# FFN2's gate and up of a hybrid decoder layer, with seven block products for eight

## The chip, the core and the metric

The kernel runs on one core of one Trainium2 chip. The metric is the device time of one execution in microseconds (us). The engines are TensorE (PE; its weight loads are listed as PEld), VectorE (DVE), ScalarE (ACT), GpSimd (POOL) and SyncE (SP), which issues the DMAs. Matmuls accumulate in PSUM; all else lies in SBUF.

## The reference

One decoder layer over 1024 tokens (and 16 meta tokens) of width 1024. The change touches the last sub-layer alone:

```python
def rms_norm(x, g):
    y = xf * lax.rsqrt(jnp.mean(xf * xf, axis=-1, keepdims=True) + EPS)
    return (y * g.astype(jnp.float32)).astype(x.dtype)
def swiglu(x, w_gate, w_up, w_down):
    return (jax.nn.silu(x @ w_gate) * (x @ w_up)) @ w_down
...
h = h + 0.5 * swiglu(rms_norm(h, g_ffn2[l]), w2_gate[l], w2_up[l], w2_down[l])
```

Gate and up are products of 1024 features, 1024 tokens and 2816 columns each; down goes back from 2816 to 1024. All is float32.

## The kernel before, in words

Features or columns lie on the 128 partitions and tokens along the free dimension, so `h` is eight tiles of 128 x 1024. Every float32 operand x of a matmul is split into a rounded part `hi` (ACT copies it to fp32r) and a rest `lo` (x - hi, a subtraction on POOL, on DVE where named), and each product is three passes (`PASS`): hi hi, hi lo, lo hi.

The layer runs FFN1, the mixer's projections, attention (in an order written out by a table of due times), the output projection (16 products `out_proj`, eight feature tiles by two token halves) and FFN2. Outside attention the framework's scheduler sets the order on each engine; the engines then run their queues strictly in that order.

FFN2 has 22 column blocks of 128 for gate and up. `FFN.gu` makes one block for one half of the tokens (chunk c, 512 tokens) with 24 matmuls of 512 columns: three passes over eight feature tiles (line 289). Its input u is h times the gain g, split in `scaled_u` (line 207 on ACT, 208 on DVE). The norm's factor 1/rms of each token comes later: `gate` multiplies the PSUM result by it (line 301), takes silu (302) and multiplies by the factor again for up (303, POOL); `up` multiplies up's result with that (317) and splits the product (318, 319). Since the factor comes late, the first blocks need only h. `rstd_cols` and `rstd_rows` make it: small matmuls with ones (line 218), a chain of tiny DVE operations (225, 135 to 142), a copy (236), four transposes on PE (240) and a copy (241).

`down` (line 327) takes two blocks at a time: for each of eight output tiles and two halves, six matmuls, then one DVE operation that adds half of it to h (line 333). Weights come as whole blocks of 512 KB (line 174, SP's queue) and are split whole, 128 x 1024 (182 on ACT, 183 on POOL; the same lines split the output projection's weights).

Three other lines are named in the rows: 198 sums the squares of h on POOL, 1218 adds an `out_proj` result in PSUM to h on DVE, and 1113 makes a `lo` part in attention on DVE from two SBUF tensors.

Of the kernel before, what the change touches and what calls it, by code (L numbers as in the profile page):

```python
# [1405 lines left out]


# [75 lines left out]
```

## Time and profile before

| | us |
|---|---|
| three runs | 2260.83, 2263.03, 2263.74 |
| median of the runs | 2263.03 |
| profiled execution, its own time | 2260.83 |
| profiled execution, span from first to last instruction | 2259.1 |

The profiled execution is the fastest of the three runs; 1.73 us of its time lie outside the span. The page gives PE 97% of the span, DVE 41%, ACT 30% and POOL 36%. In the stretches FFN1 fills the time to about 780 us, the projections to about 1060, attention to about 1430, the output projection to about 1520, and FFN2 the rest. Times in the rows are us from the span's start; PEclk is the clock that TensorE was granted, 1.00 being full speed.

### The profile page before, as it was taken

To read this page: it belongs to the slowest core of one execution; us is meant where nothing else is said; L and a number is where in the kernel's file an instruction comes from. 1 tells how busy PE (TensorE), PEld (TensorE's weight loads), DVE (VectorE), ACT (ScalarE), POOL (GpSimd) and SP (SyncE) were. 2 spreads that over 40 slices of the span, in tenths; PEclk is the share of its full clock that TensorE was granted. 3 is DMA by queue.
4 is the path that set the end of the run, shared out by engine and by line. 5 is a ranking of instruction groups with operands and counts; after the bars stand their busy time and mean duration, and the time that the engine had idled before them with its cause. 6 is when DMAs were issued, how large, how long until landed. Compare 5 with 4: busy or idle time off the path is not lost.

```text
span 2259.1 us, 29231 instructions
## 1 busy us (share of the span) xinstructions
PE 2181.1 (97%) x11667; PEld 1881.2 (83%) x11667; DVE 926.1 (41%) x1933; ACT 676.4 (30%) x1181; POOL 817.1 (36%) x609
## 2 busy tenths in 40 slices
PE   7999999999999979988988999999999999999999
PEld 7999999999999967856666777778888888888887
DVE  8332222232223776654666776273222222222222
ACT  5211211111211443332665777342111111111110
POOL 4433433333433621421332223374433333433331
PEclk9999999999999999998998999999999999999999
DMA  4111111111110114354332212231111111111101
GB/s 161 57 53 41 57 38 56 38 38 57 57 38 30 40 38 116 111 193 149 115 107 64 58 49 89 65 103 47 55 39 56 37 38 56 56 47 47 47 19 75
DMA packets 96095, 149.10 MB, mean 66 GB/s; under 512 B 25512, under 2 KB 66056, under 8 KB 95960
## 3 DMA queue, kind: packets, MB, share of 16 engines
q1 hardware_dynamic: 95672, 147.12, 19.9%
q8 instruction: 91, 1.49, 0.3%
q14 instruction: 44, 0.36, 0.0%
q10 hardware_dynamic: 288, 0.13, 0.0%
HBM read 119.32 MB, written 27.77 MB: 65 GB/s over the span
## 4 chain that ended last, share of the span: by engine, by line
PE 87%; DVE 5%; DMA 5%; ACT 2%; issue 1%; SPq 0%; POOL 0%; DVEq 0%; ACTq 0%; POOLq 0%
PE t L289 11%; PE s L289 11%; PE m L289 11%; PE o L289 10%; PE m L327 5%; PE t L327 5%; PE o L327 5%; PE s L327 5%; PE s L549 5%; PE o L1134 4%; PE s L1086 3%; DMA b<-q_f 2%; PE m L1009 2%; PE t L549 1%; DVE b L208 1%
## 5 line engine op out<-in xcount | busy, mean ns | idle before, releaser
L183 POOL TENSOR_TENSOR b<-b,b 128x1024 fp32r<-128x1024 f32 (+2 forms) x161 | 387.1, 2412 | 705.7 <-ACT b L182 698.2
L182 ACT ACTIVATE b<-b 128x1024 fp32r<-128x1024 f32 (+2 forms) x166 | 172.3, 1051 | 626.1 <-PE t L327 210.3
L289 PE MATMUL s<-b,b 128*128 128x512 f32 (+3 forms) x1368 | 267.0, 351 | 9.8 <-DVE b L205 9.8
L289 PE MATMUL t<-b,b 128*128 128x512 f32 (+3 forms) x1368 | 268.1, 351 | 0.2
L289 PEld LDWEIGHTS s<-b,b 128*128 128x128 f32 x1368 | 234.1, 190 | 33.4 <-ACT b L182 8.2
L289 PEld LDWEIGHTS t<-b,b 128*128 128x128 f32 x1368 | 234.0, 188 | 25.1 <-DVE b L208 0.7
L289 PE MATMUL m<-b,b 128*128 128x512 f32 (+3 forms) x1272 | 251.1, 353 | 0.0
L289 PE MATMUL o<-b,b 128*128 128x512 f32 (+3 forms) x1272 | 247.8, 350 | 0.0
L289 PEld LDWEIGHTS m<-b,b 128*128 128x128 f32 x1272 | 220.7, 189 | 23.0
L289 PEld LDWEIGHTS o<-b,b 128*128 128x128 f32 x1272 | 218.0, 189 | 21.9
L319 POOL TENSOR_TENSOR b<-a,b 128x512 fp32r<-128x512 f32 (+3 forms) x110 | 119.1, 1083 | 173.5 <-ACT b L318 173.5
L303 POOL TENSOR_TENSOR s<-s,b 128x512 f32<-128x512 f32 (+3 forms) x110 | 118.5, 1079 | 136.9 <-ACT s L302 136.9
L318 ACT ACTIVATE b<-a 128x512 fp32r<-128x512 f32 (+3 forms) x110 | 60.2, 548 | 304.6 <-DVE a L317 304.5
L1016 DVE TENSOR_REDUCE b<-m 128x1 f32<-128x144 f32 (+7 forms) x224 | 111.9, 507 | 92.6 <-PE m L1012 64.3
L327 PE MATMUL m<-b,b 128*128 128x512 f32 (+3 forms) x666 | 146.2, 350 | 0.0
L327 PE MATMUL t<-b,b 128*128 128x512 f32 (+3 forms) x660 | 143.7, 350 | 0.0
L327 PE MATMUL o<-b,b 128*128 128x512 f32 (+3 forms) x654 | 142.3, 350 | 1.3 <-DVE rv L225 1.3
L327 PE MATMUL s<-b,b 128*128 128x512 f32 (+3 forms) x660 | 142.1, 350 | 0.0
L302 ACT ACTIVATE s<-s 128x512 f32<-128x512 f32 (+3 forms) x110 | 60.2, 549 | 266.7 <-DVE s L301 266.6
L1086 PE MATMUL s<-b,b 70*128 70x512 f32 (+4 forms) x480 | 129.5, 377 | 6.1 <-ACT b L1101 3.8
L549 PE MATMUL s<-b,b 128*128 128x512 f32 (+3 forms) x504 | 124.4, 399 | 7.1 <-DVE t L615 3.6
L1111 POOL TENSOR_TENSOR s<-b,b 128x512 fp32r<-128x512 f32 (+2 forms) x48 | 59.2, 1233 | 180.2 <-ACT b L1105 115.4
(323 smaller groups left out, 3104.2 us busy)
## 6 DMA issues: line engine op xcount, KB each, us to landing
b<-in_w1g_dram SPq DMA_DIRECT2D x22, 512.0 KB
b<-in_w1u_dram SPq DMA_DIRECT2D x22, 512.0 KB
b<-in_w1d_dram SPq DMA_DIRECT2D x22, 512.0 KB
b<-in_w2g_dram SPq DMA_DIRECT2D x22, 512.0 KB
b<-in_w2u_dram SPq DMA_DIRECT2D x22, 512.0 KB
b<-in_w2d_dram SPq DMA_DIRECT2D x22, 512.0 KB
b<-in_wout_dram SPq DMA_DIRECT2D x16, 512.0 KB
b<-in_winf_dram SPq DMA_DIRECT2D x12, 512.0 KB
```

The source lines that it names most:

```text
L182: nc.scalar.activation(out=hi[:, :n], in_=raw[:, :n], func=ACTF.Copy)
L183: (eng or nc.gpsimd).tensor_tensor(out=lo[:, :n], in0=raw[:, :n], in1=hi_of(hi[:, :n]), op=ALU.subtract)
L289: nc.tensor.matmul(p[:, :w], lhsT=wt[a][:, kd, :], rhs=self.u[b][kd][:, c0:c0 + w], start=(n == 0), stop=(n == 23))
L302: nc.scalar.activation(out=s[:, :w], in_=s[:, :w], func=ACTF.Silu)
L303: nc.gpsimd.tensor_tensor(out=s[:, :w], in0=s[:, :w], in1=r, op=ALU.mult)
L318: nc.scalar.activation(out=ah, in_=a[:, :w], func=ACTF.Copy)
L319: nc.gpsimd.tensor_tensor(out=al, in0=a[:, :w], in1=hi_of(ah), op=ALU.subtract)
L327: nc.tensor.matmul(p[:, :w], lhsT=self.tiles["d", f][a][:, dc * 128:(dc + 1) * 128], rhs=self.act[f][b][:, c0:c0 + w], start=(n == 0), sto ...
L549: nc.tensor.matmul(p[:rows, :n], lhsT=u[b][2 * j + k][:, c0:c0 + rows], rhs=wt[g, j][a][:, k, :n], start=(i == 0), stop=(i == 23))
L1016: nc.vector.tensor_reduce(smax[n % 2][:, i, z:z + 1], s[:, :w], axis=AX.X, op=ALU.max)
L1086: nc.tensor.matmul(s[:, o:o + w], lhsT=kb[:kk, kc:kc + 128], rhs=qa[:kk, q0:q0 + w], start=(z == 0), stop=end and not mw)
L1134: nc.tensor.matmul(O[:rows, c], lhsT=v, rhs=hl[p][:r, o:o + w], start=(k == 0 and z == 0), stop=(end and z == 2))
```

## The change

FFN2 no longer uses `FFN`. Its input is normalised first: `unorm` multiplies h, gain and factor (two SBUF tensors on DVE), and the result is split like any operand. The token halves are U11 and U12 for the first four feature tiles, U21 and U22 for the last four.

Column blocks 0 and 1 are made as before, 24 matmuls each for a half (`plain`). From block 2 on `chain` takes two blocks f, f+1 at a time as a 2 x 2 problem: two column blocks, two halves of the features, two halves of the tokens. Seven products of 12 matmuls (three passes over four feature tiles) take the place of eight, in the Winograd form of Strassen's scheme: the weight sums are S1 = W21 + W22, S2 = S1 - W11, S3 = W11 - W21, S4 = W12 - S2; the input sums are T1 = U12 - U11, T2 = U22 - T1, T3 = U22 - U12, T4 = U21 - T2, each split into hi and lo. The input sums are made once; the weight sums for each pair of blocks. The seven results are put together by seven additions on DVE for each of gate and up (one of them begins as a copy on ACT).

Weights come as quarters of 128 x 512 (256 KB) into four raw buffers; a quarter is loaded when the one four before it has been used up. An operand of a product is split (128 x 512) into one of four slots when the product four before it is done. The down weights share both.

```diff
-    CH2 = [(0, 512), (512, 512)]
-    uu = ([oh[k] for k in range(KD)], [ol[k] for k in range(KD)])
-    rbc2 = blk(37)
-    ffn2 = FFN(h, uu, CH2, oring, (w2g, w2u, w2d), [(28, 29), (38, 39), (43, 44)],
-               rbc2, ps)
...
+    REG, RAWB, ACTB = [28, 29, 38, 39], [43, 44], [40, 41, 42, 45]
+    TB = ([24, 25, 26, 27], [30, 31, 32, 33], [34, 35, 36, 37])
...
+    def split2(hi, lo, src, eng=None):
+        nc.scalar.activation(out=hi, in_=src, func=ACTF.Copy)
+        (eng or nc.gpsimd).tensor_tensor(out=lo, in0=src, in1=hi_of(hi), op=ALU.subtract)
+    def dsub(out, a, b):
+        nc.vector.tensor_tensor(out=out, in0=a, in1=b, op=ALU.subtract)
...
+    def unorm(out, k, c):
+        nc.vector.scalar_tensor_tensor(out=out, in0=h[k][:, 512 * c:512 * c + 512],
+                                       scalar=gc[:, G_FFN2 + k:G_FFN2 + k + 1], in1=rbc[c],
+                                       op0=ALU.mult, op1=ALU.mult)
+    def half0(k):
+        t = ht("t", bufs=3)
+        unorm(t, k, 0)
+        split2(*u_half(k, 0), t)
...
+        def plan(self, items):
+            for key, slot in items:
+                k, f, z = key
+                if slot is None:
+                    slot = REG[self.turn % 4]
+                    self.at[key] = self.turn
+                    self.turn += 1
+                self.items.append((key, slot))
+                if k == "d" or f < 2:
+                    self.loads.append(key)
+                    self.uses[key] = 1
...
+        def load_ahead(self):
+            while self.nl < len(self.loads):
+                n = self.nl
+                if n > 3 and self.uses[self.loads[n - 4]]:
+                    return
...
+        def source(self, key):
+            k, f, z = key
+            q = lambda n: self.use(k, f, n)
+            if z == "S1":
+                t = self.sums[k, f, z] = ht("acc")
+                nc.vector.tensor_tensor(out=t, in0=q(21), in1=q(22), op=ALU.add)
+            elif z == "S2":
+                t = self.sums[k, f, z] = ht("acc")
+                dsub(t, self.sums[k, f, "S1"], q(11))
+                w = self.sums[k, f, "S3"] = q(11)
+                dsub(w, w, q(21))
+            elif z == "S3":
+                q(11)
+            elif z == "S4":
+                w = self.sums[key] = q(12)
+                dsub(w, w, self.sums[k, f, "S2"])
+            else:
+                return q(z)
+            return self.sums[key]
...
+        def done(self, key):
+            t = self.at[key] + 4
+            for i, (k, _) in enumerate(self.items):
+                if self.at.get(k) == t:
+                    self.split_to(i + 1)
...
     for k in range(len(EC["OP"]), 16):
         o_split(k + 3)
         o_load(k + 5)
-        if k > 13:
-            ffn2.split_to(k - 13)
         out_proj(k, ps)
-        if k >= 8:
-            scaled_u(h, k - 8, 0, 512, G_FFN2, *uu)
+        if k == 8:
+            y0 = rstd_cols(ps, 512, accs[0])
         if k == 9:
-            rstd_rows(ps, 0, 512, rstd_cols(ps, 512, accs[0]), rbc2)
-    for kd in range(KD):
-        scaled_u(h, kd, 512, 512, G_FFN2, *uu)
-    ffn2.split_to(4)
...
-    ffn2.run(first2, last2)
+            normal(0, y0)
+        if 9 <= k < 15:
+            for kd in ((0, 4), (1, 5), (2,), (6,), (3,), (7,))[k - 9]:
+                half0(kd)
+        if k == 12:
+            W = Weights()
+            W.plan([((m, f, z), None if f == 0 else TB[2][2 * (m == "u") + (z == 12)])
+                    for f in (0, 1) for m in "gu" for z in (11, 12)])
+            W.load_ahead()
+        if k > 12:
+            W.split_to(k - 12)
+    W.split_to(4)
...
+    def mms(p, a, bs, first, last):
+        n = 0
+        for x, y in PASS:
+            for j in range(4):
+                nc.tensor.matmul(p, lhsT=a[x][:, j, :], rhs=U[bs, j][y],
+                                 start=first and n == 0, stop=last and n == 11)
+                n += 1
...
+    def chain(m, f):
+        st = {}
+        PR = {1: (11, 11), 5: ("S1", "T1"), 6: ("S2", "T2"), 2: (12, 21), 7: ("S3", "T3"),
+              3: ("S4", 22), 4: (22, "T4")}
...
+        def add(out, p, t):
+            nc.vector.tensor_tensor(out=out, in0=p, in1=t, op=ALU.add)
+        def step(n):
+            p = st[n] = ps()
+            wk, uk = PR[n]
+            mms(p, W.op[m, f, wk], uk, True, True)
+            W.done((m, f, wk))
+            if n == 1:
+                nc.scalar.activation(out=place(0, 0), in_=p, func=ACTF.Copy)
+            elif n == 6:
+                add(place(0, 1), p, st[0, 0])
+            elif n == 2:
+                add(st[0, 0], p, st[0, 0])
+                post(0, 0)
+            elif n == 7:
+                add(place(1, 0), p, st[0, 1])
+                add(st[0, 1], st[5], st[0, 1])
+                add(place(1, 1), st[5], st[1, 0])
+                post(1, 1)
+            elif n == 3:
+                add(st[0, 1], p, st[0, 1])
+                post(0, 1)
+            elif n == 4:
+                add(st[1, 0], p, st[1, 0])
+                post(1, 0)
+        return step
...
+    OPS = (11, "S1", "S2", 12, "S3", "S4", 22)
+    for f in range(0, NF, 2):
+        if f:
+            W.plan([(("g", f, z), None) for z in OPS])
+            W.plan([(("d", f - 2 + i, z), None) for z in (0, 1) for i in (0, 1)])
+            W.plan([(("u", f, z), None) for z in OPS])
...
+    plain("g", 0, 0)
+    y1 = rstd_cols(ps, 512, accs[1])
+    W.split_to(6)
+    plain("u", 0, 0)
+    normal(1, y1)
...
+    for j in range(4):
+        unorm(b12[j], j, 1)
+        unorm(b22[j], j + 4, 1)
+        split2(*U[12, j], b12[j])
+        split2(*U[22, j], b22[j], nc.vector)
+    W.split_to(8)
+    plain("g", 1, 0)
+    plain("u", 1, 0)
+    for m, f in (("g", 1), ("u", 1), ("g", 0), ("u", 0)):
+        plain(m, f, 1)
+        if f == 0:
+            W.done((m, 0, 11))
+            W.done((m, 0, 12))
+        if (m, f) == ("g", 1):
+            for j in range(4):
+                for x in (0, 1):
+                    dsub(b12[j], b12[j], hi_of(U[11, j][x]))
+                U["T1", j] = hf(blk(TB[0][j], F32R))
+                split2(*U["T1", j], b12[j])
+                dsub(b22[j], b22[j], b12[j])
+        if (m, f) == ("u", 1):
+            for j in range(4):
+                U["T2", j] = hf(blk(TB[2][j], F32R))
+                split2(*U["T2", j], b22[j])
+            for z in (0, 2):
+                t3 = [ht("t", bufs=3) for _ in range(2)]
+                for j in (0, 1):
+                    dsub(t3[j], b22[z + j], hi_of(U[11, z + j][0]))
+                    dsub(t3[j], t3[j], hi_of(U[11, z + j][1]))
+                for j in (0, 1):
+                    U["T3", z + j] = hf(blk(TB[1][z + j], F32R))
+                    split2(*U["T3", z + j], t3[j])
+    for j in range(4):
+        t4 = ht("t", bufs=3)
+        dsub(t4, hi_of(U[21, j][0]), hi_of(U["T2", j][0]))
+        nc.vector.tensor_tensor(out=t4, in0=t4, in1=hi_of(U[21, j][1]), op=ALU.add)
+        dsub(t4, t4, hi_of(U["T2", j][1]))
+        U["T4", j] = u_half(j, 1)
+        split2(*U["T4", j], t4)
+    for f in range(2, NF, 2):
+        for m in "gu":
+            if m == "u":
+                for dc in range(KD):
+                    for c in (0, 1):
+                        down(f - 2, dc, c)
+                    if dc % 4 == 3:
+                        for i in (0, 1):
+                            W.done(("d", f - 2 + i, dc // 4))
+                acts()
+            step = chain(m, f)
+            for n in (1, 5, 6, 2, 7, 3, 4):
+                step(n)
...
+    W.split_to(len(W.items))
+    for c in (1, 0):
+        for dc in range(KD):
+            down(NF - 2, dc, c)
+            nc.sync.dma_start(out=outT[dc][:, 512 * c:512 * c + 512],
+                              in_=h[dc][:, 512 * c:512 * c + 512])
```

Lines of the changed kernel that the order's rows name: 1389 and 1390 are the two operations of `split2`, 1393 is `dsub`, 1402 `unorm`, 1465 the sum S1, 1527 the matmuls of `mms`, 1552 up's product in `plain`, 1613 and 1617 down and its addition.

On DVE, from the copy of the second token half's factor (line 241) on; before, where the blocks 0 and 1 are put together and down begins (b37 is the factor, b0 to b4 are h):

```order
L241 COPY b37_13779<-m_14465 128x512
L301 TENSOR_TENSOR s_14601<-s_14491,b37_13779 128x512
L317 TENSOR_TENSOR a_14605<-o_14516,s_14601 128x512
L301 TENSOR_TENSOR s_14609<-t_14551,b37_13779 128x512
L317 TENSOR_TENSOR a_14613<-m_14576,s_14609 128x512
L301 TENSOR_TENSOR s_14654<-s_14629,b37_13779 128x512
L333 SCALAR_TENSOR_TENSOR b0_86<-o_14664,b0_86 128x512
L333 SCALAR_TENSOR_TENSOR b0_86<-t_14672,b0_86 128x512
```
Now (acc_14428 is the factor, b30 to b33 hold the normalised half, b8 to b15 the hi parts of u, b20 to b23 lo parts, acc_14706 S2):

```order
L241 COPY acc_14428<-o_14431 128x512
L1465 TENSOR_TENSOR acc_14673<-b44_14220 128x512
L1402 SCALAR_TENSOR_TENSOR b30_14437<-b0_86,gc_73,acc_14428 128x512
L1402 SCALAR_TENSOR_TENSOR b32_14439<-b4_90,gc_73,acc_14428 128x512
L1402 SCALAR_TENSOR_TENSOR b30_14437<-b1_87,gc_73,acc_14428 128x512
L1402 SCALAR_TENSOR_TENSOR b32_14439<-b5_91,gc_73,acc_14428 128x512
L1402 SCALAR_TENSOR_TENSOR b31_14438<-b2_88,gc_73,acc_14428 128x512
L1402 SCALAR_TENSOR_TENSOR b33_14440<-b6_92,gc_73,acc_14428 128x512
L1402 SCALAR_TENSOR_TENSOR b31_14438<-b3_89,gc_73,acc_14428 128x512
L1402 SCALAR_TENSOR_TENSOR b33_14440<-b7_93,gc_73,acc_14428 128x512
L1552 TENSOR_TENSOR s_14498<-m_14500,s_14498 128x512
L1390 TENSOR_TENSOR b20_9787<-b32_14439,b12_9786 128x512
```
In place of operations that read PSUM and one SBUF tensor there stand here, and for 41 more rows, almost only operations on two SBUF tensors.

On POOL at the same place, before (s and a are the gate's and up's results, b25 to b36 raw weights):

```order
L303 TENSOR_TENSOR s_14481<-s_14481,b37_13779 128x512
L319 TENSOR_TENSOR b39_14486<-a_14487,b38_14485 128x512
L183 TENSOR_TENSOR b45_14622<-b36_14549,b42_14621 128x1024
L303 TENSOR_TENSOR s_14601<-s_14601,b37_13779 128x512
L183 TENSOR_TENSOR b41_14659<-b24_14625,b40_14658 128x1024
L319 TENSOR_TENSOR b29_14476<-a_14605,b28_14475 128x512
L183 TENSOR_TENSOR b31_14729<-b25_14627,b30_14728 128x1024
L303 TENSOR_TENSOR s_14609<-s_14609,b37_13779 128x512
```
Now (b16 to b19 are lo parts of u's second half, b24 to b27 T1, b34 on T2):

```order
L1390 TENSOR_TENSOR b16_11785<-b30_14437,b8_11784 128x512
L1390 TENSOR_TENSOR b17_12347<-b30_14437,b9_12346 128x512
L1390 TENSOR_TENSOR b18_12909<-b31_14438,b10_12908 128x512
L1390 TENSOR_TENSOR b19_13446<-b31_14438,b11_13445 128x512
L1390 TENSOR_TENSOR b45_14343<-s_14498,b42_14342 128x512
L1390 TENSOR_TENSOR b24_14557<-b30_14437,b24_14557 128x512
L1390 TENSOR_TENSOR b25_14563<-b30_14437,b25_14563 128x512
L1390 TENSOR_TENSOR b26_14569<-b31_14438,b26_14569 128x512
L1390 TENSOR_TENSOR b27_14575<-b31_14438,b27_14575 128x512
L1390 TENSOR_TENSOR b34_14607<-b32_14439,b34_14607 128x512
L1390 TENSOR_TENSOR b36_14613<-b33_14440,b36_14613 128x512
L1390 TENSOR_TENSOR b35_14610<-b32_14439,b35_14610 128x512
```
The splits of the input and its sums stand in a row here; the weights of the first pair follow them, among T3 and T4.

On PE, around the end of the first pair's gate products and the first down; before, the last of up's block 1 and down's first product:

```order
L289 MATMUL s_14629<-b14_10727,b35_14544 128x512
L289 MATMUL s_14629<-b15_11231,b35_14544 128x512
L327 MATMUL o_14664<-b28_14475,b26_14617 128x512
L327 MATMUL o_14664<-b38_14485,b42_14621 128x512
L327 MATMUL o_14664<-b29_14476,b26_14617 128x512
L327 MATMUL o_14664<-b39_14486,b42_14621 128x512
```
Now (t_14857 is the product of W22 and T4, s_14815 that with T3, m_14876 and the like are down's):

```order
L1527 MATMUL s_14815<-b32_14637,b28_14752 128x512
L1527 MATMUL s_14815<-b33_14640,b28_14752 128x512
L1527 MATMUL o_14838<-b12_9786,b29_14772 128x512
L1527 MATMUL o_14838<-b13_10259,b29_14772 128x512
L1527 MATMUL o_14838<-b14_10727,b29_14772 128x512
L1527 MATMUL o_14838<-b15_11231,b29_14772 128x512
L1613 MATMUL m_14876<-b40_14340,b39_14809 128x512
L1613 MATMUL s_14884<-b40_14340,b39_14809 128x512
L1613 MATMUL t_14900<-b40_14340,b39_14809 128x512
L1613 MATMUL m_14908<-b40_14340,b39_14809 128x512
L1527 MATMUL t_14857<-b10_12908,b38_14790 128x512
L1613 MATMUL s_14916<-b40_14340,b39_14809 128x512
```
The product with T4 is spread among down's matmuls; its last part begins 42 rows further on.

## Rows read from the trace of the kernel before

**Rows 1.** The page, part 1: busy time of each engine.

```profile
PE 2181.1 (97%) x11667; PEld 1881.2 (83%) x11667; DVE 926.1 (41%) x1933; ACT 676.4 (30%) x1181; POOL 817.1 (36%) x609
```

**Rows 2.** Chain of waits, 1520 to 1760: start us, us, what.

```profile
1660.59 5.57 PE o L289 x24
...
1705.09 1.39 PE o L327 x6
...
1727.37 5.56 PE o L289 x24
```

**Rows 3.** Chain of waits, 2150 to 2260, its end.

```profile
2253.92 1.40 PE m L327 x6
...
2255.35 0.69 DVE b L333
```

**Rows 4.** Busy time by stretch, 1800 to 1867; columns as in the first line.

```profile
core 0: us, PE busy (x) PEld busy (x) DVE busy (x) ACT busy (x) POOL busy (x), PEclk, DMA share, GB/s
...
1800.00:1867.00 67.00, 67.00 (x291) 54.44 (x290) 16.94 (x25) 11.19 (x14) 24.57 (x14) 1.00 0.14 48
```

**Rows 5.** Groups by shape, POOL, 1520 to 2260: line, operation, shapes, count | busy, mean ns | idle.

```profile
L183 POOL TENSOR_TENSOR b<-b,b 128x1024 fp32r<-128x1024 f32 x61 | 146.7, 2412 | 310.7 <-ACT b L182 308.5 <-issue 2.2
...
L319 POOL TENSOR_TENSOR b<-a,b 128x512 fp32r<-128x512 f32 x44 | 56.9, 1294 | 78.0 <-ACT b L318 78.0
```

**Rows 6.** Groups by shape, DVE, 1520 to 2260.

```profile
L333 DVE SCALAR_TENSOR_TENSOR b<-t,b 128x512 f32<-128x512 f32 x44 | 30.4, 691 | 37.6 <-PE t L327 37.6
...
L301 DVE TENSOR_TENSOR s<-s,b 128x512 f32<-128x512 f32 x22 | 15.2, 691 | 103.4 <-PE s L289 103.4
```

**Rows 7.** Timeline of DVE, 1399 to 1400.5: start us, us, what.

```profile
1399.73 0.69 DVE L1113 TENSOR_TENSOR a<-b,b 128x512 fp32r<-128x512 f32 x1 [0.59 <-ACT b L1105]
```

**Rows 8.** Groups by shape, ACT, 1520 to 2260.

```profile
L182 ACT ACTIVATE b<-b 128x1024 fp32r<-128x1024 f32 x61 | 63.7, 1058 | 316.5 <-PE s L327 201.5 <-PE t L289 46.6 <-DMA b<-in_w2u_dram 40.0
...
L318 ACT ACTIVATE b<-a 128x512 fp32r<-128x512 f32 x44 | 27.6, 628 | 135.7 <-DVE a L317 135.7
```

**Rows 9.** Timeline of SP, 1603 to 1610.

```profile
1607.67 0.33 SPq L174 DMA_DIRECT2D b<-in_w2u_dram  x1
```

**Rows 10.** Timeline of ACT, 1608 to 1612.

```profile
1610.83 1.06 ACT L182 ACTIVATE b<-b 128x1024 fp32r<-128x1024 f32 x1 [4.31 <-DMA b<-in_w2u_dram]
```

**Rows 11.** Timeline of DVE, 1477.6 to 1487.

```profile
1477.66 8.53 DVE L208 SCALAR_TENSOR_TENSOR b<-b,gc,b 128x512 fp32r<-128x512 f32 x4
1486.12 0.68 DVE L1218 TENSOR_TENSOR b<-s,b 128x512 f32<-128x512 f32 x1
```

**Rows 12.** Timeline of POOL, 1477.6 to 1487.

```profile
1478.26 2.84 POOL L183 TENSOR_TENSOR b<-b,b 128x1024 fp32r<-128x1024 f32 x1
1481.06 1.74 POOL L198 TENSOR_TENSOR acc<-acc,t 128x512 f32<-128x512 f32 x1
1482.76 2.88 POOL L183 TENSOR_TENSOR b<-b,b 128x1024 fp32r<-128x1024 f32 x1
1485.61 1.75 POOL L198 TENSOR_TENSOR acc<-acc,t 128x512 f32<-128x512 f32 x1
```

**Rows 13.** Busy time by stretch, 1404 to 1416.

```profile
1404.00:1406.00 2.00, 0.16 (x1) 0.00 (x0) 2.00 (x3) 1.97 (x4) 1.18 (x1) 1.00 0.14 25
...
1408.00:1410.00 2.00, 2.00 (x14) 1.86 (x14) 1.04 (x1) 0.71 (x2) 0.86 (x1) 0.50 0.63 174
...
1412.00:1414.00 2.00, 2.00 (x7) 1.33 (x6) 0.61 (x1) 0.60 (x1) 0.00 (x0) 0.50 0.00 0
```

**Rows 14.** Chain of waits, 1395 to 1525, first normalisation of FFN2.

```profile
1489.65 0.80 PE t L218 x8
...
1500.03 0.66 PE m L240 x4
```

**Rows 15.** Busy time by stretch, 1480 to 1500.

```profile
1480.00:1500.00 20.00, 18.45 (x84) 14.80 (x82) 17.16 (x21) 5.89 (x7) 18.24 (x10) 1.00 0.32 106
```

**Rows 16.** Timeline of DVE, 1537 to 1542, second normalisation.

```profile
1537.90 0.16 DVE L225 TENSOR_SCALAR rv<-o 128x4 f32<-128x4 f32 x1
...
1541.28 0.43 DVE L236 COPY t<-ry 128x512 f32<-128x512 f32 x1
```

**Rows 17.** Timeline of POOL, 1400 to 1600.

```profile
1446.70 1.29 POOL L1178 TENSOR_TENSOR b<-t,b 64x512 fp32r<-64x512 f32 x1 [10.96 <-ACT b L1174]
```

More of the change, by code (lines that the diff above doesn't have):

```diff
@@ L1372, in hymba_kernel, with u_half, hf @@
             f_(*a)
-    CH2 = [(0, 512), (512, 512)]
-    uu = ([oh[k] for k in range(KD)], [ol[k] for k in range(KD)])
-    rbc2 = blk(37)
-    ffn2 = FFN(h, uu, CH2, oring, (w2g, w2u, w2d), [(28, 29), (38, 39), (43, 44)],
-               rbc2, ps)
+    REG, RAWB, ACTB = [28, 29, 38, 39], [43, 44], [40, 41, 42, 45]
+    TB = ([24, 25, 26, 27], [30, 31, 32, 33], [34, 35, 36, 37])
+    def u_half(k, c):
+        return [x[k][:, 512 * c:512 * c + 512] for x in (oh, ol)]
+    def hf(x):
+        return [x[:, 0:512], x[:, 512:1024]]
@@ new lines, in split2, with normal @@
+    def split2(hi, lo, src, eng=None):
[3 more added lines that the diff above has]
+        nc.vector.tensor_tensor(out=out, in0=a, in1=b, op=ALU.subtract)
+    rbc = [None, None]
+    def normal(c, cols):
+        rbc[c] = ht("acc")
+        rstd_rows(ps, 0, 512, cols, rbc[c])
+    def unorm(out, k, c):
+        nc.vector.scalar_tensor_tensor(out=out, in0=h[k][:, 512 * c:512 * c + 512],
+                                       scalar=gc[:, G_FFN2 + k:G_FFN2 + k + 1], in1=rbc[c],
+                                       op0=ALU.mult, op1=ALU.mult)
@@ new lines, in half0, with __init__, use, split_to @@
+    def half0(k):
+        t = ht("t", bufs=3)
+        unorm(t, k, 0)
+        split2(*u_half(k, 0), t)
+    class Weights:
+        def __init__(self):
+            self.raw = [v for b in RAWB for v in hf(blk(b))]
+            self.nl = self.ns = self.turn = 0
+            self.loads, self.items = [], []
+            self.uses, self.where, self.op, self.sums, self.at = {}, {}, {}, {}, {}
+        def plan(self, items):
[9 more added lines that the diff above has]
+                    self.uses[key] = 1
+                elif z == 11:
+                    for q, n in ((11, 4), (12, 2), (21, 2), (22, 2)):
+                        self.loads.append((k, f, q))
+                        self.uses[k, f, q] = n
+        def load_ahead(self):
[3 more added lines that the diff above has]
+                    return
+                k, f, z = self.loads[n]
+                if k == "d":
+                    src = w2d[f][:, 512 * z:512 * z + 512]
+                else:
+                    i, j = divmod(z, 10)
+                    src = (w2g if k == "g" else w2u)[f + (i - 1) * (f > 1)]
+                    src = src[:, 4 * (j - 1):4 * j, :]
+                raw = self.where[k, f, z] = self.raw[n % 4]
+                nc.sync.dma_start(out=raw, in_=src)
+                self.nl += 1
+        def use(self, *key):
+            self.load_ahead()
+            self.uses[key] -= 1
+            return self.where[key]
+        def source(self, key):
[14 more added lines that the diff above has]
+                dsub(w, w, self.sums[k, f, "S2"])
+            else:
+                return q(z)
+            return self.sums[key]
+        def split_to(self, n):
+            while self.ns < min(n, len(self.items)):
+                key, slot = self.items[self.ns]
+                self.ns += 1
+                src = self.source(key)
+                hi, lo = hf(blk(slot, F32R))
+                split2(hi, lo, src)
+                self.op[key] = [x.rearrange("p (a b) -> p a b", a=4) for x in (hi, lo)]
+                self.load_ahead()
+        def done(self, key):
[3 more added lines that the diff above has]
+                    self.split_to(i + 1)
@@ L1401, in last2 @@
-    def last2(c, dc):
-        c0, w = CH2[c]
-        nc.sync.dma_start(out=outT[dc][:, c0:c0 + w], in_=h[dc][:, c0:c0 + w])
-    ffn2.run(first2, last2)
+            normal(0, y0)
[7 more added lines that the diff above has]
+            W.load_ahead()
@@ new lines, in hymba_kernel @@
+        if k > 12:
+            W.split_to(k - 12)
+    W.split_to(4)
+    U = {}
+    for j in range(4):
+        U[11, j], U[21, j] = u_half(j, 0), u_half(j + 4, 0)
+        U[12, j], U[22, j] = u_half(j, 1), u_half(j + 4, 1)
+    def mms(p, a, bs, first, last):
[5 more added lines that the diff above has]
+                n += 1
@@ new lines, in hymba_kernel, with acts, act_out, plain @@
+    act = {}
+    def acts():
+        for f in range(2):
+            b = [blk(ACTB[2 * f + x], F32R) for x in range(2)]
+            for c in range(2):
+                act[f, c] = [x[:, 512 * c:512 * c + 512] for x in b]
+    def act_out(f, c, a):
+        split2(*act[f, c], a)
+    def plain(m, f, c):
+        p = ps()
+        for z in (1, 2):
+            mms(p, W.op[m, f, 10 + z], 10 * z + c + 1, z == 1, z == 2)
+        if m == "g":
+            s = sil[f, c] = ht("sa"[c])
+            nc.scalar.activation(out=s, in_=p, func=ACTF.Silu)
+        else:
+            a = sil.pop((f, c))
+            nc.vector.tensor_tensor(out=a, in0=p, in1=a, op=ALU.mult)
+            act_out(f, c, a)
@@ new lines, in hymba_kernel, with place, post @@
+    sil = {}
+    def chain(m, f):
+        st = {}
+        PR = {1: (11, 11), 5: ("S1", "T1"), 6: ("S2", "T2"), 2: (12, 21), 7: ("S3", "T3"),
+              3: ("S4", 22), 4: (22, "T4")}
+        def place(i, c):
+            if m == "g":
+                t = sil[i, c] = ht("sa"[c])
+            else:
+                t = ht("t", bufs=3)
+            st[i, c] = t
+            return t
+        def post(i, c):
+            t = st[i, c]
+            if m == "g":
+                nc.scalar.activation(out=t, in_=t, func=ACTF.Silu)
+            else:
+                s = sil.pop((i, c))
+                nc.vector.tensor_tensor(out=s, in0=t, in1=s, op=ALU.mult)
+                act_out(i, c, s)
+        def add(out, p, t):
[24 more added lines that the diff above has]
+        return step
@@ new lines, in down @@
+    def down(f, dc, c):
+        p = ps()
+        n = 0
+        for x, y in PASS:
+            for i in (0, 1):
+                nc.tensor.matmul(p, lhsT=W.op["d", f + i, dc // 4][x][:, dc % 4, :],
+                                 rhs=act[i, c][y], start=(n == 0), stop=(n == 5))
+                n += 1
+        hc = h[dc][:, 512 * c:512 * c + 512]
+        nc.vector.scalar_tensor_tensor(out=hc, in0=p, scalar=0.5, in1=hc, op0=ALU.mult,
+                                       op1=ALU.add)
+    OPS = (11, "S1", "S2", 12, "S3", "S4", 22)
@@ new lines, in hymba_kernel @@
+    for f in range(0, NF, 2):
[3 more added lines that the diff above has]
+            W.plan([(("u", f, z), None) for z in OPS])
+    W.plan([(("d", NF - 2 + i, z), None) for z in (0, 1) for i in (0, 1)])
+    acts()
[4 more added lines that the diff above has]
+    normal(1, y1)
+    tmp = [blk(b) for b in TB[1]]
+    b12, b22 = ([v for t in tmp[i:i + 2] for v in hf(t)] for i in (0, 2))
@@ new lines, in hymba_kernel @@
+    for j in range(4):
+        t4 = ht("t", bufs=3)
[11 more added lines that the diff above has]
+                    if dc % 4 == 3:
+                        for i in (0, 1):
+                            W.done(("d", f - 2 + i, dc // 4))
+                acts()
+            step = chain(m, f)
+            for n in (1, 5, 6, 2, 7, 3, 4):
+                step(n)
```

5 lines of the change are left out of this document (removed).

## The prediction

> **What bounds the kernel now.** The page's first part comes first [rows 1]: PE is busy 97% of the span, no other engine over 41%. The chain of waits is read next, in FFN2 [rows 2]: it is one PE piece after another. Up or gate of one block and one half, 24 matmuls, takes 5.57 us, down's six take 1.39; both give 0.2317 us a matmul. A pair of column blocks runs from 1660.59 to 1727.37: 66.78 us for its 288 matmuls (192 of gate and up, 96 of down), with nothing between them. The chain ends with a matmul and one DVE operation [rows 3]. In a stretch of one pair's length [rows 4] DVE works 16.94 us of 67, ACT 11.19, POOL 24.57, and the clock is 1.00. So here a matmul less is 0.2317 us less, as long as the others keep up.
>
> **The matmuls that go.** Blocks 2 to 21 are ten pairs, with gate and up. A product has 12 matmuls, so 7 x 12 = 84 replace 96: 10 x 2 x 12 = 240 go. The program of PE has 240 fewer, so that the change does what it says is not in doubt. 240 x 0.2317 = 55.6 us. A pair then has 264 matmuls, 61.2 us.
>
> **What comes instead, in a pair of the steady part.** POOL: before, six whole splits at 2.41 and eight operations of 512 at 1.29 [rows 5], 24.8 us (the window has 24.57); now 14 + 4 splits and 4 products' lo parts, 22 x 1.29 = 28.4. DVE: 16 additions for down, 14 that put products together (these read PSUM), 8 weight sums and 4 multiplications (these read two SBUF tensors), 42 x 0.69 [rows 6, 7] = 29.0. ACT: 18 splits, 4 of the product, 4 silu and 2 copies at 0.63 [rows 8], 17.6. All are under 61.2. Lateness matters more than load: an operand gets its slot when the product four before it is done, so it has three products, 8.3 us, for 0.69 + 0.63 + 1.29 = 2.6 us of work, or some 4 with another in front of it. The tightest transfer is the last quarter of gate's weights behind up: its buffer is free about 10 us after up's chain starts, landing takes at most the 3.2 us that a block of twice the size took from issue [rows 9] to its split [rows 10], and the product that needs it starts 22 us after the chain's start. That leaves over 5 us once its sum and split are made. I take 0 for the ten pairs; below nothing is excluded (PE has no gap to give back), and above I allow 1 us a pair, 10 in all.
>
> **The start, where cover is short.** What matters is how DVE and POOL go together. Alone, a DVE operation on two SBUF tensors of 512 takes 0.69 [rows 7], as does one that reads PSUM [rows 6]. At 1477.66 four of line 208 (two SBUF tensors each) took 8.53, or 2.13 each [rows 11], while POOL did four operations in the same time [rows 12]: one of DVE to one of POOL. POOL's were longer too: 2.84 and 2.88 for 2.41, 1.74 and 1.75 for the 1.29 of a like one. Line 1218, which reads PSUM, took its usual 0.68 at 1486.12 with POOL busy. So the two wait for each other, each DVE operation on two SBUF tensors adding 0.46 to a POOL operation of 512: together 1.75 for the two.
>
> The changed order puts such work in a heap behind the second copy of the factor (line 241). From there to the lo part of T4's last tile the rows of the two queues hold 48 DVE operations on two SBUF tensors (8 of `unorm`, 4 lo parts, 8 + 4 + 8 + 12 that make T1 to T4, 4 weight sums) and 33 of POOL (4 lo parts of U12, 16 of T1 to T4, 10 of weights, 3 of products). Thirty-three pairs at 1.75 are 57.8 us, the other 15 of DVE at 0.69 are 10.4: 68.1 us from the end of that copy.
>
> PE's cover: 11 matmuls stand between the transposes (line 240) and the first that needs the second half, 217 more stand between that one and the first that needs the last lo part of T4 (gate's products, and down's first ones, are already spread out there to fill). The copy takes 0.69 beside the first of the 11, so PE would be there 11 x 0.2317 - 0.73 = 1.8 us after its end, plus 217 x 0.2317 = 50.3: 52.1. The wait is 68.1 - 52.1 = 16.0 us, spread over several places, as T1, T2, T3 come late in turn. Bounds: with no mutual hindrance POOL alone, the longer queue, needs 33 x 1.29 = 42.6, which is hidden, so 0 (less than nothing is excluded: no matmul more goes); with no overlap at all 42.6 + 48 x 0.69 = 75.7, a wait of 23.6. I take 16, since the rows show just this mixture of operations.
>
> The Trainium skill (SBUF — State Buffer, section "SBUF: two separate sides") speaks against the change here: a VectorE operation with two SBUF inputs and a GpSimd operation share a port pair, "an exclusive lock, not a bandwidth split", held for the whole instruction. By that rule the wait would be the 23.6 of the upper bound; the trace agrees that they exclude each other, but has 1.75 for two [rows 12], less than 1.29 + 0.69 = 1.98, so I keep to the rows.
>
> A wait of PE can also cost its clock: after a pause with 0.16 us busy of 2, the granted clock stood at 0.50, its lower level of 1.2 GHz, from 1408 to 1414 [rows 13]. Some 7 us at half speed cost 3.7. In this stretch PE waits anyway, so I take 0 and keep 0 to 3.7.
>
> **The first half's normalisation.** Before, PE ran dry at the factor's chain, 1489.65 to 1500.03 [rows 14]: its DVE part was held up by POOL, and PE lost 20 - 18.45 = 1.55 us there [rows 15]. Now 34 matmuls, 7.9 us, stand between lines 218 and 240, they come some 4 us later, when POOL has little to do, and without the eight operations of line 208 ahead. Undisturbed the chain took 1541.71 - 1537.90 = 3.8 us [rows 16]. I take 1.5 us back; at the worst it stays as it was. The next step, eight `unorm` and their splits, is 15 POOL operations and 8 of DVE from about 1504: 15 x 1.29 + 8 x 0.46 = 23 us, done at 1527; PE reaches the matmul that needs its end near 1528. I take 0, bound 0 to 3. The second half's chain has 38 matmuls, 8.8 us, over it: 0. The end: one half of down is done first while the last lo part is made, and several products are begun with their hi parts, so 0, bound 2. Loads of FFN2's first weights now go out before the last of the output projection's, but in a stretch where POOL and the queue idle (POOL waited 10.96 us before 1446.70 [rows 17]): 0.
>
> **Sum.** 2259.1 - 55.6 - 1.5 + 16.0 = 2218.0 of span, with 1.7 outside it 2219.7. The profiled execution lies 2.2 under the median of the runs, so against that median 2221.9. I predict 2221, between the two.
>
> **Rivals.**
> 1. No wait at the start: DVE and POOL overlap, or the mixture is milder than at 1477. Then 2219.7 - 16 = 2204. For it: in the steady part DVE keeps 0.69 on the mean [rows 6] with POOL working over a third of the time; against it: those operations read PSUM.
> 2. Full exclusion and a clock that drops behind it, 7.6 + 3.7 us more, and some lateness in the pairs: 2231 to 2241. By the rule of the Trainium skill alone it would be 2227.
> 3. Slower than before: operands come late in the chains, PE waits, and the clock falls each time. The tightest place is up's chain: 11 POOL operations and 8 of DVE on two SBUF tensors, 11 x 1.29 + 8 x 0.46 = 17.9 of its 19.5 us. A lag of more than the 4 us of slack there would make PE wait. Such an event costs 2 us and 3.7 of clock, 5.7 [rows 13]; gate's chain shares its lag, so up to twenty events, 114 us: 2334. It decides from eight events on (55.6 + 1.5 - 16 = 41 us). Against it: the gate chain and down behind it have 11.6 and some 6 us of POOL work in 19.5 and 22.2, where a lag is made good.
>
> **How the numbers follow.** The forecast (a wait of 8 to 23 us) has 0.64, with its own range 2211 to 2228; rival 1 0.14; rival 2 0.16; rival 3 with a gain that is lost 0.06, of which 0.04 is slower. The range 2206 to 2240 leaves out half of rival 1, a little of rival 2 and all of rival 3. What a measurement tells from no change is 0.2%, 4.5 us: faster 0.94, the same 0.02, slower 0.04.
>
> **What would show it.** In the new profile: 264 matmuls and 61.2 us from one pair to the next; in the heap behind the second line 241, lines 1393, 1390 and 1402 on DVE over 1.2 us on the mean and POOL's 1390 over 1.5, and 60 to 76 us from that copy to T4's last lo part, PE with 12 to 20 us idle in it; no gap at the first line 240. The forecast is wrong if those means are 0.7 and 1.3 with PE full (rival 1), or if the pairs lie over 62 us apart (rival 3).

## The result, and the profile after

| | us |
|---|---|
| before, median of 4 runs | 2262.91 (2260.83 to 2263.74) |
| after, median of 4 runs | 2225.00 (2223.64 to 2226.09) |
| ratio | 0.9834, 95% interval 0.9817 to 0.9851 |
| profiled execution after: own time, span | 2223.64, 2221.9 |

The forecast was 2221, the range 2206 to 2240. The wait at the start and the clock behind it cost more than forecast, and the 4 us come from that.

The page's first part of the changed kernel answers to [rows 1]: PE has 240 matmuls fewer, DVE, ACT and POOL have more.

```profile
PE 2130.6 (96%) x11427; PEld 1838.4 (83%) x11427; DVE 1102.3 (50%) x2145; ACT 742.6 (33%) x1343; POOL 923.2 (42%) x719
```

PE's busy time fell by 50.5 us, not by 55.6: the matmuls that are left got slower somewhere. The busy time of one pair's stretch (columns as in [rows 4]), and two pieces of the chain of waits at its ends (start us, us, what), answer to [rows 2, 4].

```profile
1666.17:1727.21 61.04, 61.04 (x266) 49.60 (x265) 32.35 (x42) 16.85 (x28) 30.70 (x22) 1.00 0.15 52
```
```profile
1666.17 1.39 PE o L1613 x6
...
1727.21 1.38 PE m L1613 x6
```

From one pair to the next it is 61.04 us, PE has no gap, and the clock is 1.00; from 1666 to 2154 it is 61.04 eight times over. The saving in the steady part is whole. The loss lies at the start of FFN2. Busy time of PE by stretch (length, busy us and matmuls, granted clock, DMA share, GB/s):

```profile
1480.00:1500.00 20.00, 20.00 (x92) 1.00 0.04 14
...
1520.00:1540.00 20.00, 20.00 (x94) 1.00 0.04 13
1540.00:1550.00 10.00, 7.53 (x25) 0.86 0.01 2
1550.00:1560.00 10.00, 10.00 (x43) 0.97 0.00 0
...
1570.00:1580.00 10.00, 7.67 (x32) 1.00 0.08 26
1580.00:1590.00 10.00, 5.37 (x21) 1.00 0.01 2
1590.00:1600.00 10.00, 7.23 (x24) 0.83 0.16 52
1600.00:1610.00 10.00, 7.78 (x28) 0.83 0.32 105
1610.00:1620.00 10.00, 10.00 (x45) 1.00 0.07 26
```

The first row answers to [rows 15]: PE is full where it had lost 1.55 us. From 1540 to 1610 it idles 2.47 + 2.33 + 4.63 + 2.77 + 2.22 = 14.4 us. Its matmuls are slower there too: 25 take 7.53 us in the stretch from 1540, where 45 take 10 at full clock.

What remains when nothing waits follows from before: FFN2 took 2259.1 - 1520.42 = 738.7 us from its first matmul to the end, less 55.6 is 683.1. After, it took 2221.9 - 1518.16 = 703.7. The loss is 20.6 us: 14.4 idle, 6.2 in slow matmuls. (By the sum of spans, -37.2 = -55.6 - 1.55 + 14.4 + x, the slow ones cost 5.6; by PE's busy time on the page 5.1. The expectations below speak of 5.1 and of 19.5 in all.) This counts PE's time and names no cause: a slow matmul ahead of a later wait only makes that wait shorter, if the end of the wait does not hang on PE.

What PE waited for last is the end of the heap. DVE at its start and there (start us, us, engine, line, operation, operands, idle before):

```profile
1539.42 0.69 DVE L241 COPY acc<-o 128x512 f32<-128x512 f32 x1 [4.30 <-PE o L240]
...
1540.63 8.49 DVE L1402 SCALAR_TENSOR_TENSOR b<-b,gc,acc 128x512 f32<-128x512 f32 x8
...
1599.93 1.63 DVE L1672 TENSOR_TENSOR t<-t,b 128x512 f32<-128x512 f32 x1
1601.48 0.68 DVE L1581 TENSOR_TENSOR s<-s,a 128x512 f32<-128x512 f32 x1
```
The heap in the chain of waits, its first rows and its last:

```profile
1538.95 0.45 PE o L240 x4
...
1539.42 0.06 DVE acc L241
...
1601.56 0.61 DVE s L1581
1602.17 0.04 issue
1602.22 0.80 PE s L1613
```
POOL's last operation on T4, and PE behind its last wait:

```profile
1605.57 1.30 POOL L1390 TENSOR_TENSOR b<-t,b 128x512 fp32r<-128x512 f32 x1
```
```profile
1602.22 0.80 PE L1613 MATMUL s<-b,b 128*128 128x512 f32 x1 [2.81 <-DVE s L1581]
1602.81 1.48 PE L1613 MATMUL m<-b,b 128*128 128x512 f32 x3
1604.09 1.40 PE L1613 MATMUL s<-b,b 128*128 128x512 f32 x3
1605.33 0.86 PE L1613 MATMUL t<-b,b 128*128 128x512 f32 x3
```

T4's last lo part is ready at 1606.87, 66.8 us after line 241's copy ended at 1540.11 (forecast 68.1). But PE needs it at 1613.58 only. Its last wait ended at 1602.22, on a PSUM tile: line 1581 adds up a finished product and so frees it, and this operation, which takes part in no exclusion (0.68 us with POOL busy), stood in DVE's queue behind T4's sums (line 1672 in 1.63 us). That is 62.1 us after the end of line 241's copy, and 182 matmuls start between the two, 42 us at 0.2317.

Between 1539.42 and 1602.17 the chain names DVE, POOL and ACT and no matmul. By it, nothing that PE did in between, slow matmuls included, moved the end of the last wait. Behind that wait the clock is low once more: seven matmuls take 3.11 us, from 1602.22 to 1605.33, where seven at 0.2317 take 1.62. So 1.5 us of the loss are slow matmuls that add to it; the other 19.1 are how late PE was at 1602.22, and the slow matmuls before that stand where PE would have waited.

### The profile page after: what moved, and what is told of

Read it like the earlier page. It is cut to its first block, busy times and chain, and to the rows that moved or that the text cites. A ratio compares the mean times of both kernels' runs of the same rounds, so it can differ in the third digit from the quotient of the medians.

```text
span 2221.9 us, 29635 instructions
## 1 busy us (share of the span) xinstructions
PE 2130.6 (96%) x11427; PEld 1838.4 (83%) x11427; DVE 1102.3 (50%) x2145; ACT 742.6 (33%) x1343; POOL 923.2 (42%) x719
## 3 DMA queue, kind: packets, MB, share of 16 engines
q1 hardware_dynamic: 105176, 147.12, 20.6%
## 4 chain that ended last, share of the span: by engine, by line
PE 84%; DVE 6%; DMA 4%; ACT 2%; issue 2%; POOL 1%; SPq 0%; DVEq 0%; POOLq 0%; ACTq 0%
PE s L289 6%; PE t L289 6%; PE o L289 5%; PE m L289 5%; PE t L1527 5%; PE s L549 5%; PE m L1527 4%; PE s L1527 4%; PE o L1527 4%; PE o L1134 4%; PE s L1086 3%; PE s L1613 3%; PE m L1613 3%; PE o L1613 3%; PE t L1613 3%; PE m L327 3%
## 5 line engine op out<-in xcount | busy, mean ns | idle before, releaser
L183 POOL TENSOR_TENSOR b<-b,b 128x1024 fp32r<-128x1024 f32 (+2 forms) x95 | 227.5, 2403 | 388.7 <-ACT b L182 386.9
L1390 POOL TENSOR_TENSOR b<-b,b 128x512 fp32r<-128x512 f32 x164 | 233.6, 1433 | 207.8 <-ACT b L1389 207.8
L289 PE MATMUL s<-b,b 128*128 128x256 f32 (+2 forms) x840 | 141.2, 324 | 10.1 <-ACT b L182 8.6
L289 PEld LDWEIGHTS s<-b,b 128*128 128x128 f32 x840 | 135.6, 192 | 10.5 <-ACT b L182 8.6
L289 PE MATMUL t<-b,b 128*128 128x384 f32 (+2 forms) x816 | 135.8, 321 | 0.0
L549 PE MATMUL s<-b,b 128*128 128x512 f32 (+3 forms) x504 | 123.8, 397 | 6.9 <-DVE t L615 3.8
L289 PE MATMUL o<-b,b 128*128 128x256 f32 (+2 forms) x768 | 128.5, 323 | 0.0
L289 PE MATMUL m<-b,b 128*128 128x384 f32 (+2 forms) x744 | 125.2, 324 | 0.0
L1527 PE MATMUL t<-b,b 128*128 128x512 f32 x492 | 122.9, 395 | 0.0
L1527 PE MATMUL s<-b,b 128*128 128x512 f32 x468 | 118.4, 397 | 4.2 <-ACT b L1389 2.4
L1134 PE MATMUL o<-b,b 128*66 128x512 f32 (+4 forms) x448 | 117.9, 346 | 0.0
```

What stands on the lines that cost most here:

```text
L183: (eng or nc.gpsimd).tensor_tensor(out=lo[:, :n], in0=raw[:, :n], in1=hi_of(hi[:, :n]), op=ALU.subtract)
L289: nc.tensor.matmul(p[:, :w], lhsT=wt[a][:, kd, :], rhs=self.u[b][kd][:, c0:c0 + w], start=(n == 0), stop=(n == 23))
L549: nc.tensor.matmul(p[:rows, :n], lhsT=u[b][2 * j + k][:, c0:c0 + rows], rhs=wt[g, j][a][:, k, :n], start=(i == 0), stop=(i == 23))
L1134: nc.tensor.matmul(O[:rows, c], lhsT=v, rhs=hl[p][:r, o:o + w], start=(k == 0 and z == 0), stop=(end and z == 2))
L1390: (eng or nc.gpsimd).tensor_tensor(out=lo, in0=src, in1=hi_of(hi), op=ALU.subtract)
L1527: nc.tensor.matmul(p, lhsT=a[x][:, j, :], rhs=U[bs, j][y], start=first and n == 0, stop=last and n == 11)
```

## The experiments

All are edits of the changed kernel. Loss is FFN2's length less 683.1 (688.7 where a pair is plain), idle is PE's in 1515 to 1620; the rest of the loss is slow matmuls (in e2 0.4 of it lies behind the last matmul). Both come from the one profiled execution.

| run | median us (4 runs) | ratio to before, 95% | loss | idle |
|---|---|---|---|---|
| changed kernel | 2225.00 | 0.9817 to 0.9851 | 20.6 | 14.4 |
| e1 no sums | 2208.79 | 0.9750 to 0.9783 | 4.1 | 2.6 |
| e2 lo parts on DVE | 2217.08 | 0.9790 to 0.9820 | 10.5 | 5.0 |
| e4 first pair plain | 2229.53 | 0.9846 to 0.9875 | 19.2 | 12.4 |
| e5 the same, T4 late | 2216.94 | 0.9786 to 0.9819 | 6.6 | 5.0 |
| e6 e2 and squares on DVE | 2212.02 | 0.9761 to 0.9791 | 6.9 | 5.1 |
| e7 the whole heap on DVE | 2209.31 | 0.9745 to 0.9780 | 2.5 | 2.3 |
| e8 squares on DVE alone | 2224.42 | 0.9818 to 0.9847 | 19.5 | 11.7 |

**e1.**

```diff
-    chain: (S1, T1) (S2, T2) (S3, T3) (22, T4); T1 to T4 made and split
+    chain: (S1, 12) (S2, 22) (S3, 12) (22, 21); no T is made
```


> Leaves out the four sums T1 to T4 of the input and their splits (28 DVE operations on two SBUF tensors, 16 ACT, 16 POOL); the products read U12, U22, U12 and U21 in their place, so the output is not the reference's. Every matmul stays. Theory A (the heap of DVE and POOL work behind the second line 241 is what PE waits for: 14.4 us idle and 5.1 us of matmuls at a lower clock in the changed kernel): both go, 2225 - 19.5 = 2205.5 us, PE full from 1540 on. Rival C (the first pair of column blocks is slow by itself, its weights or its PSUM tiles come late): PE still idles 5 us or more in its first chain, 2210 to 2225.

PE by stretch:

```profile
1540.00:1550.00 10.00, 7.54 (x33) 1.00 0.00 0
1550.00:1560.00 10.00, 9.88 (x36) 0.83 0.01 2
1560.00:1570.00 10.00, 10.00 (x45) 1.00 0.00 0
```
From 1560 on PE is full, the first chain included, so rival C falls. (The DVE operations left out are 8 + 4 + 8 + 12 = 32, not 28.) 16.5 of the 20.6 us belong to the sums. Theory A had them all; 4.1 belong to the step before, the eight `unorm` and splits behind line 241, which have 11 matmuls (2.5 us) as cover.

**e2.**

```diff
-            split2(*U["T1", j], b12[j])
+            split2(*U["T1", j], b12[j], nc.vector)
...the same for U12, T2, T3 and T4
```


> Moves the lo parts of U12 and of T1 to T4 (20 subtractions of 512) from POOL to DVE; nothing else. Theory A (DVE and POOL exclude each other on two SBUF operands, so that the heap is as long as the sum of both: a DVE operation at its spacing of 0.60, a POOL operation at 1.2): before 48 x 0.60 + 33 x 1.2 = 68.4, now 68 x 0.60 + 13 x 1.2 = 56.4, 12 us less, of which PE gets back some 10 to 14 with its clock: 2211 to 2215 us. Rival B (no exclusion worth speaking of; PE waits because results pass from DVE to ACT to POOL in the order of the queues, and the longest queue decides): DVE gets 20 x 0.69 = 13.8 us longer and is the longest queue, so no gain or a loss: 2225 to 2237.

Faster by 7.9 us (the slowest of its runs, 2218.78, is under the fastest of the changed kernel, 2223.64) and by 10.1 in FFN2. DVE got 20 operations more and became the longer queue, and the loss halved: rival B falls. Theory A had 10 to 14 in the median, more than came. T4's last lo part was ready 59.6 us after line 241's copy, where theory A had 56.4 and the changed kernel 66.8. A likely part of the difference is the eight DVE operations among them that read PSUM, 0.60 each, which theory A left out. The trace shows the exclusion bare. POOL, one operation that takes 1.29 us undisturbed:

```profile
1549.78 17.30 POOL L1390 TENSOR_TENSOR b<-s,b 128x512 fp32r<-128x512 f32 x1 [12.53 <-ACT b L1389]
```
DVE meanwhile, the first rows and the last ones of a run of 28 operations at 0.60:

```profile
1548.95 3.69 DVE L1390 TENSOR_TENSOR b<-b,b 128x512 fp32r<-128x512 f32 x6
1552.55 0.69 DVE L1393 TENSOR_TENSOR acc<-acc,b 128x512 f32<-128x512 f32 x1
...
1565.80 0.69 DVE L1552 TENSOR_TENSOR a<-o,a 128x512 f32<-128x512 f32 x1
1566.40 1.22 DVE L1390 TENSOR_TENSOR b<-b,b 128x512 fp32r<-128x512 f32 x1
```
POOL gets in only at line 1552, which reads PSUM: 1565.80 + 1.28 is its end, 1567.08.

**e4.** Blocks 2 and 3 by plain products, 24 matmuls more.

```diff
+            if f == 2:
+                plain2(m, f)
+                continue
             step = chain(m, f)
```


> The first of the ten pairs (blocks 2 and 3) is computed by plain products again, 24 matmuls more for gate and for up together being 24 x 0.2317 = 5.6 us; the other nine pairs by seven products. The heap is unchanged, but T1 is first needed some 120 us later. Theory A: the loss of 19.5 us is only the heap's, and is now hidden: 2225 + 5.6 - 19.5 = 2211 us, PE full from 1550 on. Rival C (lateness belongs to the first chain, wherever it stands): the gap moves behind, 2225 to 2231.

Nothing came of it but the 24 matmuls, and that tells nothing for rival C: the edit left T4, which is written over U12, ahead of these products, so they read T4 for U12 and waited for the whole heap. The next run mends that.

**e5.**

```diff
             if f == 2:
                 plain2(m, f)
+                if m == "u":
+                    make_t4()
                 continue
```


> As the run with the plain first pair (blocks 2 and 3), but T4, which is written over U12, is made behind that pair's plain products; there it stood ahead of them, so that they read T4 for U12 and waited for the whole heap, and the run showed only the 5.6 us of the 24 matmuls more. Now the output is the reference's, and no product of the pair needs a T. Theory A (the loss of 19.5 us belongs to the heap, of which the sums make 16, as the run without sums showed, and the second half's eight products and splits the rest): 2208.8 + 5.6 = 2214 us (2212 to 2217), PE idle only between 1542 and 1552. Rival C (the loss belongs to the first chain of seven products wherever it stands): 2225 to 2231, with a gap at blocks 4 and 5.

2216.9, at the upper end: the loss goes from 20.6 to 6.6 with the heap unchanged, only needed later. PE is full from 1580 on, at blocks 4 and 5 too, so rival C falls here as well. What is left is the step behind line 241 and, not foreseen, 2.7 us at 1575, where the first weight's lo part came out of POOL's queue behind the sums.

**e6.**

```diff
         stats(h, dc, 512 * hf, 512, accs[hf],
+              nc.vector if hf and dc >= 4 else None)
...and e2
```


> The lo parts of U12 and T1 to T4 on DVE as before, and with them the last four sums of squares of the second half's factor (128x512, SBUF and SBUF), so that this factor is known sooner: 24 matmuls instead of 11 stand between the transposes (line 240) and the first matmul on the second half, 13 x 0.2317 = 3.0 us more cover. Theory A (the wait is heap minus cover, and each us of cover is a us): 3 us under the run with the lo parts alone, 2214 (2212 to 2216), and no idle PE between 1540 and 1552. Rival B (cover at the start does not count, since PE waits later for the operands of T3 and T4 behind the DVE queue): 2216 to 2218, the gap between 1580 and 1595 longer by what the first is shorter.

5.1 us under e2, 3.6 of them in FFN2 (0.4 of these behind the last matmul); in 1540 to 1550 PE idles 0.08 us (e2 0.55). The first operation behind line 241's copy, and in the chain the matmul at the end of PE's last wait, in e2 and then in e6:

```profile
1542.45 0.68 DVE L1465 TENSOR_TENSOR acc<-b 128x512 f32<-128x512 f32 x1
1598.67 0.50 PE t L1527
```
```profile
1534.89 0.68 DVE L1465 TENSOR_TENSOR acc<-b 128x512 f32<-128x512 f32 x1
1591.09 0.50 PE t L1527
```
From one to the other it is 56.2 us in both, and 13 matmuls more start in e6: that is theory A's 3.0 us. PE's idle time alone would have spoken for rival B, for in all it stayed (5.0 and 5.1) and only moved to the later gaps; what fell is the time in slow matmuls, by some 3. Idle time and slow matmuls ahead of the last wait take each other's place, and only their sum follows from heap and cover.

**e7.**

```diff
-                split2(hi, lo, src)
+                split2(hi, lo, src, nc.vector if key[:2] == ("g", 2) else None)
...the same for the products of blocks 0 and 1, and e6
```


> As the run with the lo parts of U12, T1 to T4 and four sums of squares on DVE, and now also the lo parts of gate's ten weights of blocks 2 and 3 and of the four products of blocks 0 and 1: POOL has nothing left to do in the heap, DVE has all of it, some 93 operations at a spacing of 0.60, 56 us. Theory A (one port's time: a POOL operation costs 1.2 of it, the same one on DVE 0.60, so 13 fewer on POOL save 13 x 0.6 = 7.8 us; T3's last lo part is then ready 71 x 0.60 = 42.6 us after line 241, PE needs it after 185 matmuls, 42.9): the 6.8 us that PE still lost there go but for 0 to 2, 2206 us (2204 to 2209). Rival B (the longest queue decides, not the port): DVE, now longer by 14 operations, 8 to 9 us, makes PE wait as long or longer, 2212 to 2220.

DVE alone, from line 241 on:

```profile
1539.04 0.69 DVE L241 COPY acc<-o 128x512 f32<-128x512 f32 x1 [2.23 <-PE o L240]
...
1540.25 5.38 DVE L1402 SCALAR_TENSOR_TENSOR b<-b,gc,acc 128x512 f32<-128x512 f32 x8
1545.55 2.49 DVE L1390 TENSOR_TENSOR b<-b,b 128x512 fp32r<-128x512 f32 x4
```
PE by stretch:

```profile
1570.00:1580.00 10.00, 10.00 (x45) 1.00 0.19 54
1580.00:1590.00 10.00, 8.23 (x35) 1.00 0.34 110
```
The eight `unorm` that took 8.49 us beside POOL take 5.38. Though DVE now works 60 us without a pause, the loss falls to 2.5, the clock stays at 1.00, and the median of 2209.31 beats both kernels. It lies 3 us above what theory A had, just outside its range, though the loss came out nearly as expected (2.5 for 0 to 2): FFN2's first matmul began at 1521 here and at 1516 in e6's profile, which no edit explains. In e1, e2, e4 and e5, where nothing is changed ahead of FFN2, it lies at 1519 to 1521, in the changed kernel at 1518.

**e8.** The squares of e6 alone.

> The changed kernel with the four last sums of squares of the second half on DVE and nothing else: the factor is known sooner, 24 matmuls instead of 11 stand between the transposes (line 240) and the first matmul on the second half. The heap keeps its length. If the loss is heap minus cover, 13 x 0.2317 = 3.0 us less than the changed kernel, 2222 (2220 to 2223.5); if cover at the start does not count, 2225 (2224 to 2227).

Only 0.6 us, which the scatter of the runs covers, and 1.1 in FFN2: by the number the second answer. The cover did come. The copy of line 241, and the end of the same last wait:

```profile
1536.35 0.69 DVE L241 COPY acc<-o 128x512 f32<-128x512 f32 x1 [3.62 <-PE o L240]
...
1601.01 0.50 PE L1613 MATMUL s<-b,b 128*128 128x512 f32 x1 [1.88 <-DVE s L1581]
```
195 matmuls start between the two and not 182, 3.0 us more. But the wait ended 64.0 us after the copy and not 62.1, which takes 1.9 back and leaves the 1.1. Why the heap got to that point later is not shown; the two engines took turns in another order. PE's idle time fell by 2.7 and its slow matmuls grew by 1.6, since the clock was at 0.50, the level of 1.2 GHz, from 1568 to 1580; the chain names no matmul there either.

```profile
1568.00:1570.00 2.00, 1.79 (x5) 0.50 0.00 0
...
1578.00:1580.00 2.00, 2.00 (x6) 0.50 0.00 0
```

## Why the prediction was right, and where it was off

- **The matmuls that go, and the pairs:** right. 240 fewer, 61.04 us for a pair (61.2), no gap of PE behind the start. POOL has 30.70 us in one (28.4), DVE 32.35 (29.0), ACT 16.85 (17.6): POOL and DVE were mis-sized by 2 to 3 us, since I priced them there as if they did not hinder each other. It cost nothing under 61 us.
- **The first half's normalisation:** right, no gap at line 240. The steps taken at 0 behind it, and the end, show no gap either.
- **The heap:** right in cause and length, 66.8 us against 68.1. e2, e6 and e7 show the cause: each gives DVE more to do and makes it the longer queue, and PE loses less than in the changed kernel. What the two cost is their spacing. A subtraction on DVE takes 0.60 (four in 2.49 us, e7); on POOL it takes 1.25 alone and 1.10 beside DVE, since fourteen pairs took 23.76 us, 1.70 each, between the last two rows here (the first has three POOL operations alone):

```profile
1572.25 3.77 POOL L1390 TENSOR_TENSOR b<-b,b 128x512 fp32r<-128x512 f32 x3
...
1577.22 1.76 POOL L1390 TENSOR_TENSOR b<-a,b 128x512 fp32r<-128x512 f32 x1
...
1600.98 1.71 POOL L1390 TENSOR_TENSOR b<-t,b 128x512 fp32r<-128x512 f32 x1
```
  So 48 x 0.60 + 33 x 1.10 to 1.25 is 65 to 70 us, and the 66.8 lie between. I had taken 1.75 for a pair and 0.69 for one of DVE, their durations.
- **The wait of 16.0:** the term that was mis-sized. PE was 19.1 us late at the end of its last wait, and not by my reckoning. I took one cover, up to T4's last lo part, 52.1 of 68.1 us. PE waited in turn for U12, for the T's, and last for a PSUM tile whose release was queued behind T4's sums; T4 itself came in time. At that place the heap's part is 62.1 us and the cover some 43. Both were taken too long, by 6 and by 9, so that 16.0 lies near 19.1 is in part luck. Without the sums 4.1 us stay in the step behind line 241 (e1), where the cover is 11 matmuls and not 228.
- **The clock, taken at 0:** 1.5 us, inside the bound of 3.7 (some 7 us at half speed would be 3.5). In the trace there are three falls, each in or behind a wait (columns as above):

```profile
1548.00:1550.00 2.00, 2.00 (x6) 0.50 0.00 0
...
1592.00:1594.00 2.00, 1.82 (x4) 0.50 0.17 55
...
1602.00:1604.00 2.00, 1.78 (x4) 0.50 0.38 130
```
  "PE waits anyway" holds for the first two: a later wait follows whose end does not hang on PE by the chain, and e2 and e6 bear that out (56.2 us in both). It does not hold for the third, which stands behind the last wait. No run was made with the clock held up.
- **The sum:** span 2221.9 against 2218.0. The wait adds 3.1 and the clock 1.5; FFN2 began 2.3 us earlier than before where 1.5 were forecast, which takes 0.8.
- **The rivals:** no wait at all is out (14.4 idle), lateness in the chains too (61.04). Exclusion holds as a mechanism. The Trainium skill (SBUF — State Buffer, section "SBUF: two separate sides") calls it an exclusive lock for the whole instruction. The trace agrees that one engine stops the other (17.30 us for one POOL operation in e2); summed by durations that gave 75.7 us, summed by spacings it is 65 to 70, with 66.8 measured.

## What to carry to other kernels

Where DVE works on two SBUF tensors beside POOL, add their times instead of taking the longer queue, and price them by their spacing: here a subtraction of 512 is 0.60 on DVE against 1.10 to 1.25 on POOL, and the run with all of it on DVE lost least. Count the cover at each place where PE waits, PSUM releases queued behind such work among them; the last place decides. Slow matmuls add to the loss only where no later wait takes them up. A one-time heap is worth as much care as a loop: 2225.00 became 2209.31 by naming another engine.

## What was not expected

One engine can keep the other out for far longer than one instruction. In the changed kernel, too, one POOL operation took 7.03 us behind a run on DVE, until line 1552, which reads PSUM, came at 1563.89:

```profile
1558.10 7.03 POOL L1390 TENSOR_TENSOR b<-b,b 128x512 fp32r<-128x512 f32 x1 [6.12 <-ACT b L1389]
```
In e5 it was the other way round: one DVE operation waited 9.32 us while POOL did its work at its undisturbed 1.30, and ended 0.5 us after POOL fell idle.

```profile
1577.12 9.32 DVE L1393 TENSOR_TENSOR t<-b,b 128x512 f32<-128x512 f32 x1 [5.63 <-POOL b L1390]
```
```profile
1584.59 1.31 POOL L1390 TENSOR_TENSOR b<-a,b 128x512 fp32r<-128x512 f32 x1
```
Elsewhere, as from 1577 to 1600 in the changed kernel, the two go one to one, 1.70 us from pair to pair. What decides between the two patterns was not tried and stays open.
